# The opening of a three-pass fp32 block kernel: load order, first-unit sums and the places of the side loads

## The chip, the cores and the metric

The kernel runs on one core of a Trainium2 chip. The metric is the device time of one execution in microseconds (us); lower is better. A measurement is the median over several runs.

## The reference

One residual layer with two branches, sequence 1024, width 2048, one batch, all in float32:

```python
mod = einsum('bd,de->be', silu(c), w_ada) + b_ada
shift, scale, gate = split(mod, 3)
h = rms_norm(x, g_pre) * (1 + scale) + shift
proj = einsum('bsd,de->bse', h, w_in)              # 2048 -> 8 x 1024
q, f, i, z, gate_b, gate_c, v_b, z_b = split(proj, 8)
y_a = rms_norm(hgrn2_chunkwise(q, log f, 1 - f, i), g_head) * silu(z)
y_b = gate_b * (causal_conv3(gate_c * v_b) + conv_b) * silu(z_b)
m_a, m_b = split(sigmoid(h @ w_merge + b_merge), 2)
out = (m_a * (y_a @ w_up_a) + m_b * (y_b @ w_up_b)) @ w_o
x = x + gate * rms_norm(out, g_post)
```

## The kernel before

Every large product runs on TensorE (PE) in Strassen-Winograd form, seven half-size products p1 to p7 instead of eight, and each of these as three matmuls of hi and lo float32r parts (`mm3`: hi·hi, hi·lo, lo·hi). The lo parts are made on VectorE (DVE) by `tensor_sub(raw, hi)` after ScalarE (ACT) has copied raw to hi: `split_w` for weights (tiles `w_hi`, `w_lo`), `split_h` for the factors made from h.

**The opening.** x comes in 16 loads of 512 KB, is normalised and transposed into 16 tiles `xT` (channels by sequence). `w_ada`'s scale and shift thirds come in 64 loads of 512 KB (`ada_raw`), 16 for each of four blocks q of 512 channels, in `ada_pair(q)`: the scale half goes through PE (`prow`, 16 matmuls with a one-column weight), the shift half through 16 DVE steps (`row_v`); small matmuls (`pa`) turn both into columns, and DVE makes `a_c` and `sh_c`, which scale and shift `xT`. `factors_a` then makes the factors of p1, p6, p2 and p7 of two channel groups g (tiles `fp`). There are eight groups, and block q feeds groups 2q and 2q+1.

**The first sweep.** 48 units (`unit_a`), each four weight loads of 512 KB (`w_raw`, in 512-byte pieces: a11, a21, a22, a12), sums S1, S2, S4 and a21 (tiles `s` and `w_raw`), and four products of 24 matmuls each: p1 (into `px`), p6 (`py`), p2 (`px` again), p7 (`py` again). `o` takes the results. The POOL queue stores S1 and S4 (`s_scr`, 512 KB each) and `o` (`u_scr`, 768 KB). Beside this run three side jobs: `factors_b` (factors for the second sweep, stored in `hb_scr`), `gate_step` (32 loads `ga_raw` of w_ada's gate third, four DVE steps into `gacc` for two of them) and `sums_o` (32 loads `wo`, sums of w_o stored in `t_scr`).

**The order.** A scheduler of the language places instructions by its own timing model, so a load written late may be issued early, and the other way round; `keep_in_program_order` fixes an instruction in the order in which it is written, and `issue_after` holds a block behind a given instruction. All loads named above stand on the queue of SyncE (SP). An engine takes its instructions strictly in the order in which they stand there. Large tiles share 38 buffers (`big`), the unit weights a ring of five (`raw`). Before the change, every third `ada_raw` load used one of four buffers of its own; the rest used `big`. Unit 0's first two products ran on groups 0 to 5, then 6 and 7; p2 and p7 followed after the last groups were ready.

The rest (second sweep of p5, p4, p3 over 48 units, the two branches, the up projections and the product with w_o) is written the same in both.

Of the kernel before, what the change touches and what calls it, by code (L numbers as in the profile page):

```python
# [26 lines left out]
def tile_hgrn2_shortconv_block(  # L27
# [48 lines left out]
    rows_c = const.tile([16, P], F32, name="rows_c")  # L76
# [1 line left out]
    rows_a = const.tile([80, P], F32, name="rows_a")
    rows_b = const.tile([49, P], F32, name="rows_b")
# [93 lines left out]
    xT = [None] * KT

    def load_x(si):
        for q in range(2):
# [1 line left out]
            nc.sync.dma_start(out=t, in_=x[si * P:(si + 1) * P, q * S:(q + 1) * S])  # L180
# [139 lines left out]
    units = [(w_in_v, (2 * j) * 1024 + i * P, (2 * j + 1) * 1024 + i * P) for i in range(NH) for j in range(4)]  # L320
    units += [(w_merge_v, 256 * m, 256 * m + P) for m in range(16)]

    def load_q(view, par, e0):
        raw = wp.tile([P, 8, P], F32, tag="raw", name="w_raw", bufs=5)
        nc.sync.dma_start(out=raw, in_=view[:, par, :, e0:e0 + P])
        return raw

    def unit_a(u):
        view, e1, e2 = units[u]
        a11, a21 = load_q(view, 0, e1), load_q(view, 0, e2)  # L330
        a22, a12 = load_q(view, 1, e2), load_q(view, 1, e1)
        o = ph.tile([P, 3, HS], F32, tag="o", name="o", bufs=2)
        s1, s2, s4 = (ph.tile([P, 8, P], F32, tag=f"s{n}", name=f"s{n}") for n in (1, 2, 4))
        px, py = ps("mm", "px"), ps("mm", "py")
        w1 = split_w(a11)
        if u:
            product(px, w1, fa["p1"])
        nc.vector.tensor_add(out=s1, in0=a21, in1=a22)
        nc.vector.tensor_sub(out=s2, in0=s1, in1=a11)
        nc.gpsimd.dma_start(out=s_scr[u][:, 0], in_=s1.rearrange("p a b -> p (a b)"))  # L340
        w6 = split_w(s2)
        if u == 0:
            for gs in (range(6), (6, 7)):
                product(px, w1, fa["p1"], pin=True, gs=gs)
                product(py, w6, fa["p6"], pin=True, gs=gs)
        nc.scalar.copy(out=o[:, 2], in_=px)
        if u:
            product(py, w6, fa["p6"])
        nc.vector.tensor_add(out=o[:, 1], in0=o[:, 2], in1=py)
        nc.vector.tensor_sub(out=s4, in0=a12, in1=s2)  # L350
        nc.gpsimd.dma_start(out=s_scr[u][:, 1], in_=s4.rearrange("p a b -> p (a b)"))
        product(px, split_w(a12), fa["p2"], more=True)
        nc.scalar.copy(out=o[:, 0], in_=px)
        nc.vector.tensor_sub(out=a21, in0=a11, in1=a21)
        product(py, split_w(a21), fa["p7"], more=True)
        nc.vector.tensor_add(out=o[:, 2], in0=o[:, 2], in1=py)
        nc.gpsimd.dma_start(out=u_scr[u], in_=o)
# [626 lines left out]
```

## Time and profile before

| | |
|---|---|
| median of 3 runs | 2771.5 us (2767.51 to 2771.66) |
| the profiled execution: time, span | 2769.2 us, 2767.5 us |
| PE busy | 2673.0 us, 97% of the span |
| DVE, ACT, POOL busy | 62%, 33%, 10% |
| opening (to the first product) | 0 to 142.04 us |
| unit 0 | 142.04 to 174.23 us |
| units 1 to 47 | 174.23 to 1213.65 us |

In the rows, L224 is line 224 of the kernel before; an arrow in brackets names what an engine waited for; the DMA share is that of the core's 16 DMA engines.

### The profile page before, as it was taken

How to read it: one execution, taken by the hardware profiler on the slowest of the kernel's cores; microseconds unless marked ns; L12 is line 12 of the kernel's file. 1: busy time of each engine (PE TensorE's matmuls, PEld its weight loads, DVE VectorE, ACT ScalarE, POOL GpSimd, SP SyncE). 2: the span in 40 equal slices, each digit the busy share in tenths (PEclk: the TensorE clock that was granted, in tenths of full speed). 3: DMA queues.
4: the chain of work that ended last, by engine and by line, in shares of the span. 5: the costliest groups of instructions: out<-in, count | busy, mean ns of one | idle time of the engine just before them, and what ended most of it. 6: DMA issues, size and time to landing. Idle time of an engine off the chain costs nothing.

```text
span 2767.5 us, 31307 instructions
## 1 busy us (share of the span) xinstructions
PE 2673.0 (97%) x11851; PEld 2152.7 (78%) x11851; DVE 1716.7 (62%) x2096; ACT 906.3 (33%) x1176; POOL 280.0 (10%) x495
## 2 busy tenths in 40 slices
PE   4889999999999999999999999999998999999997
PEld 3267878888888888888888888888885787888786
DVE  6777886754554444546666666656563666765667
ACT  4433222222222222233344444435442222232333
POOL 2012111110000000010000000002111101100000
PEclk9899999999999999999999999999998999999999
DMA  9769999985556655584444444359999569773353
GB/s 361 286 201 313 345 349 364 346 292 179 179 192 179 182 175 177 174 316 137 133 130 133 138 146 138 110 178 374 360 363 407 187 213 335 235 282 99 99 178 142
DMA packets 420071, 631.30 MB, mean 228 GB/s; under 512 B 19564, under 2 KB 281808, under 8 KB 419792
## 3 DMA queue, kind: packets, MB, share of 16 engines
q1 hardware_dynamic: 358528, 394.31, 44.7%
q0 software_dynamic: 60208, 230.78, 21.7%
q10 hardware_dynamic: 1184, 4.20, 0.4%
q8 instruction: 93, 1.52, 0.2%
q14 instruction: 58, 0.48, 0.0%
HBM read 431.04 MB, written 198.18 MB: 227 GB/s over the span
## 4 chain that ended last, share of the span: by engine, by line
PE 81%; issue 8%; DMA 7%; DVE 2%; POOL 1%; ACT 1%; DVEq 0%; POOLq 0%; ACTq 0%; SPq 0%
PE po L866 10%; PE pz L119 7%; PE pz L122 7%; PE pz L123 7%; PE px L119 6%; PE px L123 6%; PE px L122 6%; PE py L123 6%; PE py L119 6%; PE py L122 6%; PE pw L119 4%; PE pw L122 4%; PE pw L123 4%; DMA yp<-yf_scr 3%; DMA ga_raw<-in_w_ada_dram 2%
## 5 line engine op out<-in xcount | busy, mean ns | idle before, releaser
L130 ACT CAST w_hi<-w_raw 128x1024 fp32r<-128x1024 f32 (+1 forms) x296 | 290.9, 983 | 1001.6 <-PE px L122 402.5
L131 DVE TENSOR_TENSOR w_lo<-w_raw,w_hi 128x1024 fp32r<-128x1024 f32 (+1 forms) x296 | 335.7, 1134 | 273.1 <-ACT w_hi L130 263.4
L123 PE MATMUL py<-fp,w_lo 128*128 128x512 f32 x768 | 301.2, 392 | 6.9 <-DVE w_lo L131 6.9
L123 PE MATMUL px<-fp,w_lo 128*128 128x512 f32 x768 | 300.9, 392 | 5.2 <-DVE w_lo L131 5.2
L119 PE MATMUL px<-fp,w_hi 128*128 128x512 f32 x768 | 301.2, 392 | 0.0
L122 PE MATMUL py<-fp,w_hi 128*128 128x512 f32 x768 | 299.5, 390 | 1.3 <-DVE fp L136 1.3
L119 PE MATMUL py<-fp,w_hi 128*128 128x512 f32 x768 | 299.8, 390 | 0.9 <-ACT w_hi L130 0.9
L122 PE MATMUL px<-fp,w_hi 128*128 128x512 f32 x768 | 300.0, 391 | 0.0
L866 PE MATMUL po<-w_hi,lt 128*128 128x512 f32 x896 | 244.2, 390 | 0.6 <-DVE og L900 0.6
L866 PEld LDWEIGHTS po<-w_hi,lt 128*128 128x128 f32 x896 | 168.1, 188 | 37.2 <-DVE og L900 2.2
L130 ACT CAST w_hi<-s 128x512 fp32r<-128x512 f32 (+1 forms) x112 | 90.1, 805 | 285.9 <-PE py L122 245.5
L123 PEld LDWEIGHTS py<-fp,w_lo 128*128 128x128 f32 x768 | 144.5, 188 | 41.5 <-DVE w_lo L131 11.2
L123 PEld LDWEIGHTS px<-fp,w_lo 128*128 128x128 f32 x768 | 144.8, 188 | 36.9 <-DVE w_lo L131 6.5
L122 PEld LDWEIGHTS py<-fp,w_hi 128*128 128x128 f32 x768 | 144.5, 188 | 32.1 <-DVE fp L136 1.7
L122 PEld LDWEIGHTS px<-fp,w_hi 128*128 128x128 f32 x768 | 145.1, 189 | 30.8 <-issue 0.5
L119 PEld LDWEIGHTS px<-fp,w_hi 128*128 128x128 f32 x768 | 144.9, 189 | 30.8 <-issue 0.7
L119 PEld LDWEIGHTS py<-fp,w_hi 128*128 128x128 f32 x768 | 144.5, 188 | 30.8 <-ACT w_hi L130 1.3
L119 PE MATMUL pz<-fp,hi 128*128 128x512 f32 x384 | 152.5, 397 | 3.0 <-DVE d L701 3.0
L122 PE MATMUL pw<-fp,w_hi 128*128 128x512 f32 x384 | 150.8, 393 | 0.0
L119 PE MATMUL pz<-fp,w_hi 128*128 128x512 f32 x384 | 150.5, 392 | 0.0
L123 PE MATMUL pz<-fp,lo 128*128 128x512 f32 x384 | 150.4, 392 | 0.0
L119 PE MATMUL pw<-fp,w_hi 128*128 128x512 f32 x384 | 150.4, 392 | 0.0
(286 smaller groups left out, 4959.4 us busy)
## 6 DMA issues: line engine op xcount, KB each, us to landing
w_raw<-in_w_in_dram SPq DMA_DIRECT2D x160, 512.0 KB, 5.2
s_scr<-s POOLq DMA_DIRECT2D x96, 512.0 KB, 6.0
s_raw<-s_scr SPq DMA_DIRECT2D x96, 512.0 KB, 4.3
w_raw<-in_w_merge_dram SPq DMA_DIRECT2D x80, 512.0 KB, 5.7
u_scr<-o POOLq DMA_DIRECT2D x48, 768.0 KB, 7.5
ada_raw<-in_w_ada_dram SPq DMA_DIRECT2D x64, 512.0 KB, 10.8
yf_scr<-yp POOLq DMA_DIRECT2D x56, 512.0 KB, 9.0
yp<-yf_scr SPq DMA_DIRECT2D x56, 512.0 KB, 12.8
```

What stands on the lines that cost most here:

```text
L119: mm = nc.tensor.matmul(o, ah, bh, start=first, stop=False, skip_group_check=True)
L122: nc.tensor.matmul(o, ah, bl, start=False, stop=False, skip_group_check=True)
L123: nc.tensor.matmul(o, al, bh, start=False, stop=last, skip_group_check=True)
L130: nc.scalar.copy(out=hi, in_=raw)
L131: nc.vector.tensor_sub(out=lo, in0=raw, in1=hi.bitcast(F32))
L866: nc.tensor.matmul(o, a, b[:, c], start=st, stop=sp, skip_group_check=True)
```

## The change

In words: (1) a helper `load` pins the loads of x, `ada_raw`, the weights of units 0 and 1, `ga_raw` and `wo` in the order in which they are written. (2) All `ada_raw` loads of blocks 0 to 2 and three of four of block 3 use the 38 large buffers; the pool of their own falls from four to two, and small tiles (`rows_a`, `rows_b`, `rows_c`, `row_p`) share others, which pays for the memory. (3) Unit 0's loads, its S1, S2, a21 and the splits of a11, S2 and a12 (`hi3a`, `lo3a`) are written ahead of block 3's `ada_pair`; p1, p6 and p2 of unit 0 run over groups 0 to 5, then 6 and 7; its S4, p7 and stores are issued after `factors_a((6, 7))`. p2 has a PSUM tile of its own there. (4) `factors_b`, `gate_step` and `sums_o` move: `factors_b(u/2 - 1)` at units 2, 4, ... 16, issued after that unit's last sum; two gate steps at each of units 10 to 25 (before 16 to 31); `sums_o` at 26, 28, ... 40 (before 32 to 46), with the loads pinned, so that they can no longer be issued many units earlier.

```diff
+    def load(o, i):
+        tc.keep_in_program_order(nc.sync.dma_start(out=o, in_=i))
...
     def ada_load(t, q, k):
         n_ada[0] += 1
-        if n_ada[0] % 3:
+        if q < 3 or n_ada[0] % 4:
             raw = bigt(F32, "ada_raw").rearrange("p (k e) -> p k e", k=2)
         else:
-            raw = ph.tile([P, 2, HS], F32, tag="ada", name="ada_raw", bufs=4)
-        nc.sync.dma_start(out=raw, in_=w_ada_v[:, k:k + 2, t, q * HS:(q + 1) * HS])
+            raw = ph.tile([P, 2, HS], F32, tag="ada", name="ada_raw", bufs=2)
+        load(raw, w_ada_v[:, k:k + 2, t, q * HS:(q + 1) * HS])
         return raw
...
+    def unit_a(u, raws):
...
+        if u == 0:
+            v.tensor_sub(out=a21, in0=a11, in1=a21)
+            w2 = split_w(a12, out_t=(ph.tile([P, 8, P], F32R, name="hi3a", bufs=1), wp.tile([P, 8, P], F32R, tag="raw", name="lo3a", bufs=5)))
+            yield
+            p2 = ps("mm", "p2")
+            for gs in (range(6), (6, 7)):
+                for p, w, f in ((px, w1, "p1"), (py, w6, "p6"), (p2, w2, "p2")):
+                    product(p, w, fa[f], pin=True, gs=gs)
...
     for q in range(1, 4):
+        if q == 3:
+            first = unit_a(0, load_a(0))
+            next(first)
         ada_pair(q)
         factors_a((2 * q - 2, 2 * q - 1))
-    factors_a((6, 7), vec=(7,))
+    with tc.issue_after(factors_a((6, 7), vec=(7,)).ins):
+        next(first, None)
...
     for u in range(NU):
-        unit_a(u)
-        if u < 16:
-            if u % 2 == 0:
-                factors_b(u // 2)
-        elif u < 32:
-            gate_step(2 * u - 32)
-            gate_step(2 * u - 31)
-        elif u % 2 == 0:
-            sums_o((u - 32) // 2)
+        if u:
+            for _ in unit_a(u, load_a(u)):
+                pass
+        if u in range(2, 18, 2):
+            with tc.issue_after(last_sum[0]):
+                factors_b(u // 2 - 1)
+        if 10 <= u < 26:
+            gate_step(2 * u - 20)
+            gate_step(2 * u - 19)
+        elif u in range(26, 42, 2):
+            sums_o((u - 26) // 2)
```

What moves, on the engines that wait or are waited for. First SP's queue in the opening, before (each row is one kind of load, "x60" sixty in a row):

```order
L180 DMA x_0_427<-in_x_dram 128x1024
L180 DMA x_1_429<-in_x_dram 128x1024
L224 DMA ada_raw<-in_w_ada_dram 128x2x512 x4
L325 DMA w_raw<-in_w_in_dram 128x8x128 x5
L224 DMA ada_raw<-in_w_ada_dram 128x2x512 x60
L325 DMA w_raw<-in_w_in_dram 128x8x128 x21
```

and after:

```order
L119 DMA x_1_428<-in_x_dram 128x1024
L119 DMA ada_raw<-in_w_ada_dram 128x2x512 x48
L119 DMA w_raw<-in_w_in_dram 128x8x128 x4
L119 DMA ada_raw<-in_w_ada_dram 128x2x512 x16
L119 DMA w_raw<-in_w_in_dram 128x8x128 x4
L311 DMA w_raw<-in_w_in_dram 128x8x128 x45
L119 DMA ga_raw<-in_w_ada_dram 128x2x512
```

Five unit loads stood ahead of 60 `ada_raw` loads; now four stand ahead of the last 16. Within the 60, the order before was the scheduler's, and is the written one now.

Second, DVE around `a_c` of the last block (the last `row_v` step is the shift's; `a_c` needs PE's `pa`), before:

```order
L239 SCALAR_TENSOR_TENSOR row_v<-ada_raw,c_act,row_v 128x512 x6
L247 TENSOR_TENSOR a_c<-pa,cols 128x4
L249 TENSOR_TENSOR sh_c<-pa,cols 128x4
L338 TENSOR_TENSOR s_1184<-w_raw 128x1024
L248 SCALAR_TENSOR_TENSOR a_c<-a_c,cols 128x4
L339 TENSOR_TENSOR s_1185<-s_1184,w_raw 128x1024
L354 TENSOR_TENSOR w_raw<-w_raw 128x1024
L266 TENSOR_SCALAR xT_570<-xT_570,a_c,sh_c 128x1024
```

and after, where the sums stand a whole block earlier, right behind `a_c` of block 2 and among the first `row_v` steps of block 3:

```order
L252 SCALAR_TENSOR_TENSOR a_c<-a_c,cols 128x4
L331 TENSOR_TENSOR s_1025<-w_raw 128x1024
L332 TENSOR_TENSOR s_1026<-s_1025,w_raw 128x1024
L336 TENSOR_TENSOR w_raw<-w_raw 128x1024
L241 TENSOR_SCALAR row_v<-ada_raw,c_act 128x512
L134 TENSOR_TENSOR lo3a<-w_raw,hi3a 128x1024
L243 SCALAR_TENSOR_TENSOR row_v<-ada_raw,c_act,row_v 128x512
L134 TENSOR_TENSOR w_lo<-s_1026,w_hi 128x1024
```

Third, DVE in one of units 20 to 24, before (L338, L339, L350 and L354 are S1, S2, S4 and a21, L131 the lo parts of p6, p2, p7 and the next p1):

```order
L338 TENSOR_TENSOR s_4537<-w_raw 128x1024
L356 TENSOR_TENSOR o<-o,py 128x512
L354 TENSOR_TENSOR w_raw<-w_raw 128x1024
L131 TENSOR_TENSOR w_lo<-s_4393,w_hi 128x1024
L339 TENSOR_TENSOR s_4538<-s_4537,w_raw 128x1024
L350 TENSOR_TENSOR s_4539<-w_raw,s_4538 128x1024
L131 TENSOR_TENSOR w_lo<-w_raw,w_hi 128x1024
L349 TENSOR_TENSOR o<-o,py 128x512
L131 TENSOR_TENSOR w_lo<-w_raw,w_hi 128x1024 x2
```

and after, where units 21 to 23 read alike and 20 and 24 add the last sums of a gate block (the lines are now L331, L332, L347, L355 and L134, and L397 is a gate step):

```order
L331 TENSOR_TENSOR s_4597<-w_raw 128x1024
L357 TENSOR_TENSOR o<-o,py 128x512
L355 TENSOR_TENSOR w_raw<-w_raw 128x1024
L134 TENSOR_TENSOR w_lo<-s_4452,w_hi 128x1024
L332 TENSOR_TENSOR s_4598<-s_4597,w_raw 128x1024
L397 SCALAR_TENSOR_TENSOR gacc<-ga_raw,c_act,gacc 128x512
L347 TENSOR_TENSOR s_4599<-w_raw,s_4598 128x1024
L397 SCALAR_TENSOR_TENSOR gacc<-ga_raw,c_act,gacc 128x512
L134 TENSOR_TENSOR w_lo<-w_raw,w_hi 128x1024
L397 SCALAR_TENSOR_TENSOR gacc<-ga_raw,c_act,gacc 128x512 x2
L346 TENSOR_TENSOR o<-o,py 128x512
L134 TENSOR_TENSOR w_lo<-w_raw,w_hi 128x1024 x2
```

Four gate steps have come in, the first of them between S2 and S4. On SP's queue after, the two `ga_raw` loads of such a unit stand directly behind four `w_raw` loads, so behind a12, which waits for S1; the four `wo` loads later stand in the same place:

```order
L119 DMA ga_raw<-in_w_ada_dram 128x2x512 x2
L311 DMA w_raw<-in_w_in_dram 128x8x128 x4
L119 DMA wo<-in_w_o_dram 128x2x512 x4
L311 DMA w_raw<-in_w_in_dram 128x8x128 x8
L119 DMA wo<-in_w_o_dram 128x2x512 x4
```

Before, the `ga_raw` loads stood between single `w_raw` loads from the 26th after the opening on, well ahead of the gate steps.

## Rows read from the trace of the kernel before

**Rows 1.** The page: span, busy time of the engines.

```profile
span 2767.5 us, 31307 instructions
PE 2673.0 (97%) x11851; PEld 2152.7 (78%) x11851; DVE 1716.7 (62%) x2096; ACT 906.3 (33%) x1176; POOL 280.0 (10%) x495
```

**Rows 2.** PE's timeline, opening to unit 1: start, length, idle before in brackets.

```profile
72.14 3.57 PE L235 MATMUL prow<-ada_raw,c_act 128*1 128x512 f32 x4 [15.64 <-DMA ada_raw<-in_w_ada_dram]
...
136.10 3.38 PE L235 MATMUL prow<-ada_raw,c_act 128*1 128x512 f32 x4 [2.75 <-DMA ada_raw<-in_w_ada_dram]
140.15 1.05 PE L244 MATMUL pa<-ones,row_p 1*128 1x1 f32 x8 [0.66 <-ACT row_p L240]
...
142.04 0.48 PE L119 MATMUL px<-fp,w_hi 128*128 128x512 f32 x1
...
174.23 0.39 PE L119 MATMUL px<-fp,w_hi 128*128 128x512 f32 x1
```

**Rows 3.** DMA from 0 to 160 us: GB/s in 40 slices of 4 us.

```profile
GB/s 145 297 417 412 410 409 386 337 291 313 386 387 386 388 387 388 386 387 209 255 61 72 254 159 371 360 397 387 387 386 387 385 387 209 0 4 201 299 49 238
```

**Rows 4.** A wait of SP's queue, 0 to 142 us: total, times, longest.

```profile
SPq L224 <- PE prow L235: 14.8, 6, 5.3
```

**Rows 5.** DVE's timeline around the last a_c.

```profile
139.03 0.75 DVE L239 SCALAR_TENSOR_TENSOR row_v<-ada_raw,c_act,row_v 128x512 f32<-128x512 f32 x1
142.22 0.16 DVE L247 TENSOR_TENSOR a_c<-pa,cols 128x4 f32<-128x4 f32 x1 [2.43 <-PE pa L244]
...
145.89 0.81 DVE L266 TENSOR_SCALAR xT<-xT,a_c,sh_c 128x1024 f32<-128x1024 f32 x1
...
148.66 1.28 DVE L278 TENSOR_TENSOR xT<-keep,xT 128x512 f32<-128x512 f32 x2
```

**Rows 6.** Unit 0: busy time and clock; then PE's waits.

```profile
142.04:174.23 32.19, 26.05 (x98) 20.14 (x98) 26.80 (x36) 12.59 (x19) 2.73 (x5) 0.89 0.52 160
PE py L123 <- DVE w_lo L131: 2.7, 1, 2.7
PE px L123 <- DVE w_lo L131: 2.2, 1, 2.2
PE py L122 <- DVE fp L136: 1.3, 1, 1.3
```

**Rows 7.** Windows: 12 late units, then units 1 to 47.

```profile
696.50:957.60 261.10, 260.88 (x1150) 215.24 (x1149) 128.91 (x120) 61.41 (x72) 19.19 (x36) 1.00 0.59 179
174.23:1213.65 1039.42, 1031.27 (x4522) 848.19 (x4521) 617.67 (x621) 256.20 (x306) 121.99 (x229) 1.00 0.76 249
```

**Rows 8.** One late unit: PE, then SP, POOL and DVE.

```profile
754.93 0.39 PE L119 MATMUL px<-fp,w_hi 128*128 128x512 f32 x1
760.83 0.39 PE L123 MATMUL py<-fp,w_lo 128*128 128x512 f32 x1
766.27 0.39 PE L123 MATMUL px<-fp,w_lo 128*128 128x512 f32 x1
757.16 0.37 SPq L325 DMA_DIRECT2D w_raw<-in_w_in_dram  x1
758.26 0.53 POOL L357 DMA_DIRECT2D u_scr<-o  x1 [0.30 <-issue]
758.78 1.22 DVE L131 TENSOR_TENSOR w_lo<-s,w_hi 128x1024 fp32r<-128x1024 f32 x1
762.10 1.23 DVE L350 TENSOR_TENSOR s<-w_raw,s 128x1024 f32<-128x1024 f32 x1 [0.84 <-DMA w_raw<-in_w_in_dram]
```

**Rows 9.** Gate steps before: PE and DMA, 260 to 380 us; the loads' median time.

```profile
260.00:380.00 120.00, 116.97 (x509) 95.08 (x508) 99.19 (x119) 29.06 (x35) 14.60 (x27) 1.00 1.03 344
ga_raw<-in_w_ada_dram SPq DMA_DIRECT2D x31, 512.0 KB, 8.4
```

**Rows 10.** A wait of PE followed by the lower clock, unit 2.

```profile
227.77 0.69 PE L123 MATMUL py<-fp,w_lo 128*128 128x512 f32 x1 [1.98 <-DVE w_lo L131]
...
228.69 0.63 PE L122 MATMUL py<-fp,w_hi 128*128 128x512 f32 x1
```

More of the change, by code (lines that the diff above doesn't have):

```diff
@@ L75, in tile_hgrn2_shortconv_block @@
     make_identity(nc, ident)
[L76 removed]
+    rows = wp.tile([P, S], F32, tag="raw", name="rows", bufs=5)
+    rows_a, rows_b, rows_c = rows[0:80, 0:P], rows[0:49, P:2 * P], rows[0:16, 2 * P:3 * P]
     nc.scalar.dma_start(out=rows_c, in_=c[0].rearrange("(n p) -> n p", p=P))
[L78 to L79 removed]
     b_rows = b_ada[0].rearrange("(n p) -> n p", p=P)
@@ L135, in split_h @@
         eng(out=t[:, 0], in_=raw)
-        nc.vector.tensor_sub(out=t[:, 1], in0=raw, in1=t[:, 0].bitcast(F32))
+        return nc.vector.tensor_sub(out=t[:, 1], in0=raw, in1=t[:, 0].bitcast(F32))
     STAGES = ("p1", "p6", "p2", "p7", "p5", "p4", "p3")
@@ L179, in load_x @@
             t = bigt(F32, f"x_{si}_{q}")
-            nc.sync.dma_start(out=t, in_=x[si * P:(si + 1) * P, q * S:(q + 1) * S])
+            load(t, x[si * P:(si + 1) * P, q * S:(q + 1) * S])
             xrow[si][q] = t
@@ L229, in ada_pair @@
         prow = ps("aux", "prow")
-        row_p, row_v = (ph.tile([P, HS], F32, tag=t, name=t) for t in ("row_p", "row_v"))
+        row_p, row_v = o0[:, 0], ph.tile([P, HS], F32, tag="row_v", name="row_v")
         for k in range(0, KT, 2):
@@ L272, in keep_f @@
             fa[s][g] = pair(f"f{s}_{g}")
-            split_h(fa[s][g], raw, nc.scalar.copy)
+            return split_h(fa[s][g], raw, nc.scalar.copy)
         for g, b11, b12, b21, b22 in parts:
@@ L283, in factors_a @@
         for g, b11, b12, b21, b22 in parts:
-            keep_f("p7", g, b12)
+            last = keep_f("p7", g, b12)
+        return last
     def factors_b(g):
@@ L299, in factors_b, with load_q, load_a @@
             nc.gpsimd.dma_start(out=hb_scr[n][g], in_=t.rearrange("p a b -> p (a b)").bitcast(F32))
+    units = [(w_in_v, (2 * j) * 1024 + i * P, (2 * j + 1) * 1024 + i * P) for i in range(NH) for j in range(4)]
+    units += [(w_merge_v, 256 * m, 256 * m + P) for m in range(16)]
+    def load_q(view, par, e0, pin=False):
+        raw = wp.tile([P, 8, P], F32, tag="raw", name="w_raw", bufs=5)
+        (load if pin else nc.sync.dma_start)(raw, view[:, par, :, e0:e0 + P])
+        return raw
+    def load_a(u):
+        view, e1, e2 = units[u]
+        return [load_q(view, *a, pin=u < 2) for a in ((0, e1), (0, e2), (1, e2), (1, e1))]
@@ new lines, in tile_hgrn2_shortconv_block @@
+    last_sum = [None]
+    def unit_a(u, raws):
+        a11, a21, a22, a12 = raws
+        o = ph.tile([P, 3, HS], F32, tag="o", name="o", bufs=2) if u else o0
+        s1, s2 = (ph.tile([P, 8, P], F32, tag=f"s{n}", name=f"s{n}", bufs=1) for n in (1, 2))
+        s4 = ph.tile([P, 8, P], F32, tag="s4", name="s4") if u else s1
+        px, py = ps("mm", "px"), ps("mm", "py")
+        v = nc.vector
+        w1 = split_w(a11)
+        if u:
+            product(px, w1, fa["p1"])
+        v.tensor_add(out=s1, in0=a21, in1=a22)
+        v.tensor_sub(out=s2, in0=s1, in1=a11)
+        nc.gpsimd.dma_start(out=s_scr[u][:, 0], in_=s1.rearrange("p a b -> p (a b)"))
+        w6 = split_w(s2)
+        if u == 0:
[6 more added lines that the diff above has]
+                    product(p, w, fa[f], pin=True, gs=gs)
+        nc.scalar.copy(out=o[:, 2], in_=px)
+        if u:
+            product(py, w6, fa["p6"])
+        v.tensor_add(out=o[:, 1], in0=o[:, 2], in1=py)
+        v.tensor_sub(out=s4, in0=a12, in1=s2)
+        nc.gpsimd.dma_start(out=s_scr[u][:, 1], in_=s4.rearrange("p a b -> p (a b)"))
+        if u:
+            product(px, split_w(a12), fa["p2"], more=True)
+            nc.scalar.copy(out=o[:, 0], in_=px)
+        else:
+            v.tensor_add(out=o[:, 0], in0=o[:, 2], in1=p2)
+        if u:
+            v.tensor_sub(out=a21, in0=a11, in1=a21)
+        product(py, split_w(a21), fa["p7"], more=True)
+        last_sum[0] = v.tensor_add(out=o[:, 2], in0=o[:, 2], in1=py).ins
+        nc.gpsimd.dma_start(out=u_scr[u], in_=o)
@@ L318, in tile_hgrn2_shortconv_block @@
     ph = ph_pool.__enter__()
[L320 to L357, printed above, removed]
     gacc = [None]
@@ L364, in gate_step @@
         raw = bigt(F32, "ga_raw").rearrange("p (k e) -> p k e", k=2)
-        nc.sync.dma_start(out=raw, in_=w_ada_v[:, 2 * kq:2 * kq + 2, 2, eb * HS:(eb + 1) * HS])
+        load(raw, w_ada_v[:, 2 * kq:2 * kq + 2, 2, eb * HS:(eb + 1) * HS])
         if kq == 0:
@@ L390, in sums_o @@
         for t, par, c in ((b12, 0, 1), (b22, 1, 1), (b11, 0, 0), (b21, 1, 0)):
-            nc.sync.dma_start(out=t, in_=w_o_v[:, par, g, :, c, :])
+            load(t, w_o_v[:, par, g, :, c, :])
         v = nc.vector
```

2 lines of the change are left out of this document (added).

## The prediction

> **What bounds the kernel now.** I read the page first: PE is busy for 2673.0 of 2767.5 us [rows 1], so a gain can only come from the places where PE is idle or at the lower of its two clocks, 1.2 in place of 2.4 GHz. PE's timeline shows these places: all of the opening up to the first product at 142.04, and unit 0, which ends at 174.23 [rows 2]. Then the windows: twelve late units take 261.10 us, 21.76 each and with PE never idle for long, while units 1 to 47 take 1039.42, which is 16.8 more than 47 x 21.758 = 1022.6 [rows 7]. The changed lines reach no further than unit 47, and the instructions after it stay nearly in their order, so the sum has three terms: opening, unit 0, units 1 to 47.
>
> In the opening the DMA line is the view to look at [rows 3]: it should stand at some 387 GB/s as long as there is something to load, and in the six slices from 72 to 96 us it reads 209, 255, 61, 72, 254, 159. PE shows why: it waits 15.64 us, up to 72.14, for one scale load of block 1, whose matmuls it takes in order [rows 2], though loads for later steps were already there and held their buffers. SP's queue then waits for PE to free buffers, 14.8 us in six waits [rows 4].
>
> **The change, part by part.** *Load order.* The six slices moved 1010 x 4 = 4.04 MB where 6 x 387 x 4 = 9.29 MB could have moved; the missing 5.25 MB are 13.6 us at 387. With the loads in the order in which PE and DVE take them, and more of the large buffers, I expect this hole to close. Four unit loads instead of five stand ahead of the last block; one takes 1.8 us (524 KB at 291 GB/s, the slices from 32 to 40 where they ran). The store of unit 0's S1 now falls into the opening, 1.4 us (524 KB at 387). So the last `ada_raw` lands at 136.1 - 13.6 - 1.8 + 1.4 = 122.1 instead of 136.1.
>
> Can the engines follow? A block of 16 loads is 21.7 us of DMA. DVE needs for it 16 steps of 0.75 and 12 factor steps of 0.64 [rows 5], 19.7 us. Block 3 adds the six steps of unit 0 at 1.22 [rows 8], 27.0 in all, against 21.7 + 4 x 1.8 = 28.9. It fits, with 2 us to spare; that is the cover of the sums, and what they go beyond it would be paid one for one.
>
> *From the last load to the first product.* Before, 5.9 us: 3.4 of matmuls at the lower clock, 0.66 for ACT's copy, 1.9 of `pa` [rows 2]. In written order the last scale load lands one load, 1.4 us, ahead of the last shift load. At the full clock (1.7 for the matmuls) this gives 2.9 us behind the last load, at the lower one 4.6. I take 3.3, since the loads come evenly and PE is busy for two thirds of the time there. First product at 125.4, a gain of 16.6. The bounds are 20 (no hiccup at all) and 3 (the hole stays).
>
> *Unit 0.* It takes 32.2 us now, 10.4 above a late unit: 6.2 in three waits on DVE [rows 6], the rest the clock (mean 0.89). After, its sums are done before `a_c`. Groups 0 to 5 of three products are 54 matmuls, 54/96 of 21.76 = 12.2 us. Under these DVE makes the last two groups' factors: the columns 0.4, three scaling steps 1.6, 12 steps of 0.64, in all 9.7 [rows 5]. So the three waits go; if the cover were gone the whole 9.7 would stand in front of groups 6 and 7. I leave one stretch at the lower clock in (1.7): 23.5 us, a gain of 8.7. Unit 1 would begin 25.3 us earlier.
>
> *The sweep.* Before, the gate loads were issued far ahead and the side jobs spent most of the 16.8 us in units 2 to 12. After, I sum what is late in each unit; X is the start of its p1.
> - Unit 1: DVE's order puts unit 0's last sum, which needs the end of p7, ahead of unit 1's first lo part: 0.64 + 1.22, less the 0.45 that PE's first two matmuls cover, 1.4.
> - `factors_b` now starts behind a unit's last sum and puts two steps, 1.28, ahead of p6's lo part in some seven units. That part ends at 760.00 and is wanted at 760.83 [rows 8], so 0.45 remain of each: 3.2.
> - Its stores fall beside the load of a22 in units 4 and 6. No row before has this alone; bounds are nothing and a wait like that of unit 2, 1.98 [rows 10]. I take 1.5 each, nearer to that wait because the DMA share is high there: 3.0.
> - Gate units 20 to 24: a12 is issued at X + 2.2 and in at X + 7.2 [rows 8], and the first gate load stands right behind it. At the full rate it follows by 1.4, at half of it (beside the stores of POOL, issued at X + 3.3) by 2.7: X + 8.6 to 9.9, say 9.2. DVE takes strictly in order a gate step, S4, a gate step and p2's lo part, 0.75 + 1.23 + 0.75 + 1.22 = 3.9 with small overlaps 3.7. PE gets the lo part at X + 12.9 and wants it at X + 11.3 [rows 8]: 1.6 late, bounds 1.0 and 2.3. Five units: 7.8.
> - Gate units 10 to 19: here the steps are spread over the unit. Before, with six gate loads for each unit and all of them early, PE lost 3.0 us in 120 [rows 9], 0.55 for each unit. I take 0.6, ten times 6.0; bounds nothing and 1.6 each.
> - What I expect to stand as before (the gate's own small matmuls, scattered waits): an estimate of a third of the 16.8, 5.4.
> - The wait in unit 2 was followed by the lower clock (0.63 for a matmul [rows 10], 0.39 elsewhere [rows 8]). Unit 0's mean clock of 0.89 makes 3.5 us of its 32.2 [rows 6], lost in two such stretches, so 1.7 each. I allow for two: 3.4.
>
> Together 30.2, 13.4 more than before. The side loads for w_o stand behind a12 as well, but their sums come after p2's lo part and have some four us until p7's is due: nothing.
>
> **Sum.** -16.6 - 8.7 + 13.4 = -11.9, from the profiled execution's 2769.2 to 2757.3. That execution lay 2.3 below the median of 2771.5, so the forecast is 2760.
>
> On the half rate the Trainium skill has a rule: its page "DMA: Bandwidth & Descriptors", section "Queues, rings and completion order", says that each DMA engine goes round its queues packet by packet, so two busy queues would share it evenly. By that rule the gate loads come at the late end in every gate unit, and the sum would be that of the second rival, 2783. The trace agrees only in part: a12 was there 4.9 us after its issue with a store of 768 KB under way [rows 8].
>
> **The rivals.**
> First, *the gate loads are hidden anyway*: if the first of them lands by X + 7.5, DVE loses nothing in units 10 to 25. For it: a12 itself takes only 4.9 us, and the DMA share of a late unit is 0.59 [rows 7]. Against it: it can't be issued before a12, whose buffer waits for S1. The sweep then loses 30.2 - 13.8 - 1.7 = 14.7, and the time is 2744.
>
> Second, *the gate loads eat the gain*, the slower side: all 16 gate units stall as units 20 to 24 do at the late end. Their loads, held to their units, share each unit's worst stretch with a12 and 1.2 MB of stores. The two first terms gain 25.3, and the sweep without these units loses 16.4 where it lost 16.8 before; so the balance is at 25.7 for the 16 units, 1.6 for each. At 2.3 each they cost 36.8 in place of 13.8, and the time is 2783. For it: the 8.4 us that gate loads took before [rows 9]. Against it: 8.4 was with the DMA engines full.
>
> Third, *the opening doesn't gain*: the change doesn't do what it says, since buffers run out all the same (the 16 `xT` tiles and the factors hold most of the 38 by block 3) or DVE is short by more than its 2 us. Then the 13.6 us come back, and -11.9 + 13.6 gives 2773. Against it: the hole stands at blocks 1 and 2, when fewer factors are there.
>
> **How the numbers follow.** The forecast has 0.57, the first rival 0.15, the second 0.12, the third 0.13, other mishaps 0.03. The forecast's own range is 2751 to 2769, from the bounds of the gate units and of the opening. The range 2744 to 2777 reaches to the first and the third rival and leaves out the second. A measurement of this kernel can tell about 0.2%, 5.5 us, from no change. Faster by more holds in nine tenths of the forecast and in the first rival: 0.66. Within it are the rest of the forecast and most of the third: 0.20. Slower: 0.14.
>
> **What would show it.** Right: the DMA line at some 387 without a hole from 40 to 115 us; the last `prow` matmuls near 121 and the first product near 125; unit 0 without a wait on `w_lo` and near 23.5 us; the first gate step of units 20 to 24 waiting for `ga_raw`, and PE waiting 1 to 2 us for p2's `w_lo` there. Wrong: a second hole in the DMA line in block 3, a wait of PE between groups 5 and 6 of unit 0, gate units of 21.8 us, or waits there above 2 us each followed by the lower clock.

## The result, and the profile after

The changed kernel is slower: 2800.7 us (median of 4 runs, 2798.31 to 2808.02) beside 2769.5 for the kernel before in the same series (2763.51 to 2771.66), a ratio of 1.0127 with a 95% interval of 1.0109 to 1.0144. The forecast was 2760, and its range ended at 2777.

The profiled execution of the changed kernel took 2798.3 us. Its page, to be read beside [rows 1]:

```profile
span 2796.6 us, 31303 instructions
PE 2683.6 (96%) x11851; PEld 2151.1 (77%) x11851; DVE 1716.2 (61%) x2097; ACT 905.5 (32%) x1175; POOL 280.1 (10%) x495
...
PE 58%; DMA 16%; issue 10%; DVE 8%; POOL 2%; ACT 1%; SPq 1%; DVEq 0%; POOLq 0%; ACTq 0%
```

DVE works as long as before, and PE has 10.6 us more of busy time for the same 11851 matmuls: 16.0 more in units 1 to 47, less in the opening and in unit 0. The span is 29.1 longer. The last line is the chain that ended last: a sixth of it is DMA, where it was 7% before.

The DMA line of the opening, 0 to 160 us in slices of 4, answers to [rows 3]; PE's timeline then to [rows 2], DVE's to [rows 5]:

```profile
GB/s 149 318 410 410 410 409 387 388 384 389 384 386 388 386 387 388 384 388 384 376 389 387 332 287 351 390 388 397 172 393 301 151 0 4 0 6 252 27 240 123
```

```profile
121.56 2.89 PE L239 MATMUL prow<-ada_raw,c_act 128*1 128x512 f32 x4 [0.34 <-DMA ada_raw<-in_w_ada_dram]
...
129.57 1.87 PE L248 MATMUL pa<-ones,row_v 128*128 128x1 f32 x8 [3.42 <-DVE row_v L243]
131.30 0.77 PE L122 MATMUL px<-fp,w_hi 128*128 128x512 f32 x1
...
156.37 0.39 PE L122 MATMUL px<-fp,w_hi 128*128 128x512 f32 x1
...
103.84 0.16 DVE L251 TENSOR_TENSOR a_c<-pa,cols 128x4 f32<-128x4 f32 x1 [0.83 <-PE pa L248]
...
126.40 3.11 DVE L243 SCALAR_TENSOR_TENSOR row_v<-ada_raw,c_act,row_v 128x512 f32<-128x512 f32 x4
131.48 0.16 DVE L251 TENSOR_TENSOR a_c<-pa,cols 128x4 f32<-128x4 f32 x1 [1.96 <-PE pa L248]
```

The hole of 72 to 96 us is closed, and the last scale load is in by 121.56, near the 121 that was forecast. One slice, 112 to 116 us, still reads 172: SP's queue waits there for DVE to free buffers. A wait of SP's queue, 0 to 131 us:

```profile
SPq L119 <- DVE row_v L243: 22.6, 8, 9.5
```

`pa` waits 3.42 us for DVE's `row_v`, and the first product stands at 131.30: 10.7 earlier than before, not 16.6. Unit 0 ends at 156.37.

Windows: unit 0, units 1 to 47, block 3 in DVE's time, and a stretch of unit 23 (columns: length, busy PE, PEld, DVE, ACT, POOL, granted clock, DMA share, GB/s):

```profile
131.30:156.40 25.10, 25.04 (x98) 20.11 (x99) 13.22 (x22) 9.66 (x14) 0.54 (x1) 0.88 0.29 84
...
156.40:1242.85 1086.45, 1047.22 (x4521) 848.44 (x4520) 623.50 (x631) 256.50 (x307) 123.58 (x231) 0.99 0.74 240
...
103.84:131.48 27.64, 20.06 (x49) 5.35 (x48) 24.50 (x37) 12.11 (x17) 0.60 (x1) 0.81 0.77 263
...
680.00:683.40 3.40, 3.40 (x9) 2.64 (x8) 1.67 (x2) 0.00 (x0) 0.00 (x0) 0.50 0.59 167
```

Units 1 to 47 take 1086.45, which is 63.8 more than 47 x 21.758 = 1022.6; before it was 16.8 [rows 7]. 39.2 of them PE was idle, and 24.6 it was busy beyond the 1022.6 (8.7 before). Of the 24.6 the granted clock explains 6.8: it stands at its lower level in four short stretches, at 509, 680, 888 and 1059 us, and at the full clock elsewhere. Most of the rest, some 13 by PE's timeline, stands at the waits themselves: a matmul of 0.39 us begins 0.23 after the one ahead of it, but the last one ahead of a wait ends without this overlap, and the next begins some 0.34 after the first behind it. Unit by unit (from one p1 to the next): unit 1 loses 2.0, units 2 to 9 4.3, 10 to 19 13.8, 20 to 24 17.3 (27.2, 23.2, 24.1, 26.1, 25.4 us), units 25 to 40, which hold the w_o sums, 25.9, and the rest 0.5. The amount of side traffic alone doesn't do it: in the kernel before the w_o loads and sums stood in units 9 to 18, some four in each, no sum waited for its load, and units 10 to 19 lost 2.7. From the end of unit 47 on both kernels take the same, 1553.8 and 1553.9. So: opening -10.7, unit 0 -7.1, sweep +47.0, together +29.2.

The waits of units 1 to 47 (total, times, longest):

```profile
DVE s L331 <- DMA w_raw<-in_w_in_dram: 113.1, 29, 6.5
DVE s L331 <- DMA w_raw<-in_w_merge_dram: 82.0, 16, 6.9
...
DVE gacc L397 <- DMA ga_raw<-in_w_ada_dram: 35.3, 14, 5.4
DVE wo L416 <- DMA wo<-in_w_o_dram: 30.8, 8, 5.8
PE px L126 <- DVE w_lo L134: 24.9, 15, 2.6
...
PE py L126 <- DVE w_lo L134: 10.1, 21, 1.4
```

PE waits for lo parts, 36 times. DVE itself waits for gate and w_o loads, and far longer, 195 us in 45 waits, for unit weights: L331 is S1 = a21 + a22 of the next unit. How a gate step's wait reaches PE is seen in unit 23, DVE's timeline and then PE's, with the step (L397) ahead of p2's lo part (L134, at 677.26):

```profile
674.80 0.75 DVE L397 SCALAR_TENSOR_TENSOR gacc<-ga_raw,c_act,gacc 128x512 f32<-128x512 f32 x1 [3.73 <-DMA ga_raw<-in_w_ada_dram]
...
678.54 0.50 PE L126 MATMUL px<-fp,w_lo 128*128 128x512 f32 x1 [2.49 <-DVE w_lo L134]
```

Here is how S1's wait reaches PE, at the border of two units with w_o work (SP and POOL issue, DVE and PE work; rows by engine):

```profile
1014.88 0.39 PE L122 MATMUL px<-fp,w_hi 128*128 128x512 f32 x1
...
1028.33 0.50 PE L126 MATMUL px<-fp,w_lo 128*128 128x512 f32 x1 [1.23 <-DVE w_lo L134]
...
1015.86 0.37 SPq L311 DMA_DIRECT2D w_raw<-in_w_merge_dram  x1
...
1008.27 0.53 POOL L421 DMA_DIRECT2D t_scr<-wo  x1 [5.17 <-DVE wo L416]
...
1014.99 0.53 POOL L421 DMA_DIRECT2D t_scr<-wo  x1 [0.73 <-DVE wo L419]
1016.96 0.53 POOL L358 DMA_DIRECT2D u_scr<-o  x1 [1.44 <-issue]
...
1014.61 1.22 DVE L134 TENSOR_TENSOR w_lo<-w_raw,w_hi 128x1024 fp32r<-128x1024 f32 x1
...
1016.34 1.22 DVE L134 TENSOR_TENSOR w_lo<-s,w_hi 128x1024 fp32r<-128x1024 f32 x1
1023.52 1.23 DVE L331 TENSOR_TENSOR s<-w_raw 128x1024 f32<-128x1024 f32 x1 [5.96 <-DMA w_raw<-in_w_merge_dram]
...
1027.06 1.22 DVE L134 TENSOR_TENSOR w_lo<-w_raw,w_hi 128x1024 fp32r<-128x1024 f32 x1
```

A unit begins at 1014.88. At 1015.83 DVE has finished p1's lo part (1014.61 + 1.22), which frees one of the five weight buffers, and at 1015.86 SP issues a22 of the *next* unit into it. POOL has issued four stores of `t_scr` since 1008.27, three of them are still under way, one of `u_scr` follows at 1016.96, and a22 is in only at 1023.4, 7.5 us after its issue. DVE has S1 of the next unit in its queue *ahead* of the running unit's p2 lo part; it stands still for 5.96 us, then does S1, S2 and a21, and only at 1027.06 the lo part that PE's p2 wants at 1027.1. PE stops for 1.23; had a22 taken 6.3 us, it would not have stopped.

In the kernel before, S1 stood one lo part further forward, ahead of p6's, with almost no slack; a row of its trace (DVE's timeline in the late unit of [rows 8]) shows it:

```profile
755.90 1.23 DVE L338 TENSOR_TENSOR s<-w_raw 128x1024 f32<-128x1024 f32 x1 [4.12 <-DMA w_raw<-in_w_in_dram]
```

S1 waits 4.12 us for a22, which comes with no other transfer beside it (issued 751.81, landed 755.78), and p6's lo part, three steps behind S1 at 758.78, ends 0.83 ahead of its use [rows 8]. In that place whatever delays a22 by more than 0.83 goes to PE.

### The profile page after: what moved, and what is told of

Read it like the earlier page. It is cut to its first block, busy times and chain, and to the rows that moved or that the text cites. A ratio compares the mean times of both kernels' runs of the same rounds, so it can differ in the third digit from the quotient of the medians.

```text
span 2796.6 us, 31303 instructions
## 1 busy us (share of the span) xinstructions
PE 2683.6 (96%) x11851; PEld 2151.1 (77%) x11851; DVE 1716.2 (61%) x2097; ACT 905.5 (32%) x1175; POOL 280.1 (10%) x495
## 4 chain that ended last, share of the span: by engine, by line
PE 58%; DMA 16%; issue 10%; DVE 8%; POOL 2%; ACT 1%; SPq 1%; DVEq 0%; POOLq 0%; ACTq 0%
PE po L891 10%; PE pz L122 5%; PE pz L126 5%; PE pz L125 5%; DMA w_raw<-in_w_in_dram 4%; PE px L122 4%; PE px L126 4%; PE px L125 4%; PE py L126 3%; PE py L122 3%; PE py L125 3%; DMA wo<-in_w_o_dram 3%; DVE w_lo L134 3%; DMA yp<-yf_scr 3%; PE pw L122 3%
## 5 line engine op out<-in xcount | busy, mean ns | idle before, releaser
L134 DVE TENSOR_TENSOR w_lo<-w_raw,w_hi 128x1024 fp32r<-128x1024 f32 (+1 forms) x295 | 334.9, 1135 | 238.6 <-ACT w_hi L133 236.6
L331 DVE TENSOR_TENSOR s<-w_raw 128x1024 f32<-128x1024 f32 x48 | 58.8, 1225 | 195.1 <-DMA w_raw<-in_w_in_dram 113.1
```

What stands on the lines that cost most here:

```text
L134: nc.vector.tensor_sub(out=lo, in0=raw, in1=hi.bitcast(F32))
L331: v.tensor_add(out=s1, in0=a21, in1=a22)
```

## The experiments

Twelve kernels ran, in four groups, each group on one chip beside the kernel before; ratios are to the kernel before of the same group (medians 2765.9, 2766.7, 2765.9 and 2767.1). "Loss" is the time from the first product to the end of unit 47, less 48 x 21.76; it is 27.1 before and 67.1 after.

### Which part of the change costs the time

**e1_opening_only**: the changed opening and unit 0, with the loop of the kernel before and gate and w_o loads not pinned. **e2_side_jobs_only**: the other half, the kernel before with this loop and the pinned loads:

```diff
+        if u in range(2, 18, 2):
+            with tc.issue_after(last_sum[0]):
+                factors_b(u // 2 - 1)
+        if 10 <= u < 26:
+            gate_step(2 * u - 20)
+            gate_step(2 * u - 19)
+        elif u in range(26, 42, 2):
+            sums_o((u - 26) // 2)
```

Expected of e1: 

> The opening and unit 0 as in the changed kernel, the side jobs at their places before, their loads not pinned. Theory A (the loss sits in the side jobs, wherever the opening begins): the traces put the opening at -10.7 us and unit 0 at -7.1, so about 18 us below the kernel before, 2748 to 2755. Theory B (the new opening itself upsets the sweep, by a shifted phase of loads and buffers): the sweep keeps much of its 47 us, so not below the kernel before.

Measured: 2763.5, ratio 0.999 (0.998 to 1.0). First product at 131.43, loss 30.1. Half right: the loss stays near that of before, but the 18 us of opening and unit 0 come back only in part; units 1 to 47 lose some 27 where they lost 16.8, and unit 47 ends at 1206.1 instead of 1213.7. The side jobs of the first units, begun earlier, now meet units 0 to 9; PE's timeline has one wait of 5.26 us there, for a copy by ACT that stands behind one of `factors_b`:

```profile
161.88 0.80 PE L122 MATMUL px<-fp,w_hi 128*128 128x512 f32 x1 [5.26 <-ACT w_hi L133]
```

Expected of e2: 

> The opening of the kernel before, with only the side jobs of the changed kernel (new places, gate and w_o loads pinned). Theory A: the loss of the sweep comes with them, so 40 to 50 us above the kernel before, 2810 to 2820. Theory B: near the kernel before.

Measured: 2807.1, ratio 1.014 (1.012 to 1.0161), loss 68.0. The loss comes with the side jobs, whatever the opening.

**e3_not_pinned**: the changed kernel, where only this differs (and the same for `wo`):

```diff
-        load(raw, w_ada_v[:, 2 * kq:2 * kq + 2, 2, eb * HS:(eb + 1) * HS])
+        nc.sync.dma_start(out=raw, in_=w_ada_v[:, 2 * kq:2 * kq + 2, 2, eb * HS:(eb + 1) * HS])
```

> The changed kernel with its gate and w_o loads not pinned; the side jobs are written at the same places, so the scheduler issues the w_o loads some five units earlier and their sums with them, while the gate loads of units 10 to 17 stand where they stood. If the pin of the w_o loads is to blame for units 25 to 40 (26 us), these go and the time is 2765 to 2778. If the places in the code are to blame, it stays at 2795 to 2800.

Measured: 2759.8, ratio 0.9976 (0.9965 to 0.9987), loss 25.5. The w_o units lose next to nothing (1.5 in units 25 to 40), gate units 10 to 19 lose 14.2. The scheduler spreads the w_o sums one by one over units 21 to 29.

### Explanations that fall short

**e4_steps_behind_p2**: loads pinned as in the change, but gate steps and w_o sums held behind p2's lo part of their unit, so that no side step that waits for its load stands ahead of it.

```diff
+            lo_p2[0] = last_lo[0]
...
+        if jobs:
+            with tc.issue_after(lo_p2[0]):
+                for j in jobs:
+                    next(j, None)
```

> The changed kernel with the same pinned loads at the same places, but the DVE steps that use them (gate steps, w_o sums) issued only behind the lo part of p2 of the unit in which they are written, which is about a unit later than now. Theory 1 (DVE's queue: a step that waits for a late side load stands ahead of a lo part, and PE and the weight loads wait for that): units 20 to 40 lose 43 us now and should lose 10 at most, so 2758 to 2770. Theory 2 (DMA crowd: the held loads make the weight loads themselves late, whatever DVE does): at least half of the 43 us stays, 2780 or more.

Measured: 2784.1, ratio 1.006 (1.0042 to 1.0078), loss 53.0. Gate units 20 to 24 lose 1.0 together and 10 to 19 8.6; units 25 to 47 still lose some 35. There no w_o sum waits for its load any more, so waiting side steps are not the cause. The trace shows S1 at its longest wait, ahead of p6's lo part (L134, at 982.89):

```profile
980.01 1.23 DVE L334 TENSOR_TENSOR s<-w_raw 128x1024 f32<-128x1024 f32 x1 [9.07 <-DMA w_raw<-in_w_merge_dram]
```

Its a22 was issued at 970.97 and landed at 979.89, beside `t_scr` stores issued from 964.7 to 969, three of them still under way. So I suspected the burst of stores, or the pinned burst of w_o loads, and tried each alone on e4: **e5_stores_two_and_two** issues two of the four stores a unit later, with the order of POOL's stores fixed (its w_o loads then slip between weight loads); **e6_wo_loads_free** takes the pin from the w_o loads.

```diff
+            if n == 2:
+                yield
+            tc.keep_in_program_order(nc.gpsimd.dma_start(out=t_scr[n][g], in_=t.rearrange("p a b -> p (a b)")))
```

> The kernel of e4 with the four stores of a w_o sum split: two at their place, two held on POOL's queue until the S4 store of the next unit; the scheduler also lets two of the four w_o loads slip between the next weight loads. In e4 units 26 to 41 still lose some 35 us, and in its trace a22 takes 8.9 us in a unit with the four stores of 512 KB, 4 to 6 in one without. Theory S (the burst of stores delays a22): the loss halves or better, 2758 to 2770. Theory L (the four loads behind a12 do it): as e6. Neither: stays at 2780.

> The kernel of e4 with only the w_o loads not pinned: two of four slip between weight loads, the sums and the burst of four stores stay behind p2's lo part. Theory L (the bunch of loads behind a12): the 35 us of units 26 to 41 go for the most part, 2752 to 2762. Theory S (the burst of stores): they stay, 2775 to 2785.

Measured: e5 2784.8, ratio 1.0057 (1.004 to 1.0074), loss 58.1; e6 2807.3, ratio 1.0147 (1.0132 to 1.0162), loss 71.2. Both were missed. In e6 the w_o loads are issued among the next unit's weight loads, and the odd units from 31 to 41 take 28.4 to 30.3; a22 takes 11.5 us (issued 986.11, landed 997.62), and S1 and PE wait longer than in any other run. A wait of e6, units 0 to 47, and the row of that S1:

```profile
PE px L126 <- DVE w_lo L134: 35.5, 12, 6.8
```

```profile
997.70 1.23 DVE L334 TENSOR_TENSOR s<-w_raw 128x1024 f32<-128x1024 f32 x1 [8.78 <-DMA w_raw<-in_w_merge_dram]
...
1001.23 1.22 DVE L134 TENSOR_TENSOR w_lo<-w_raw,w_hi 128x1024 fp32r<-128x1024 f32 x1
```

**e7_gate_held_wo_free**: the gate as in e4, w_o as in e3.

> The best version that the runs so far point to: the gate loads pinned and their steps behind p2's lo part as in e4, the w_o sums as in e3 (not pinned, not held). The gate units 10 to 25 lost 9 us in e4 against 14 in e3, the w_o units nothing in e3; so 4 to 6 us below e3, 2752 to 2757, if the two are independent; at e3's 2760 or above if the w_o sums, now later than in e3, meet the just-in-time loads of units 24 to 35.

Measured: 2763.5, ratio 0.9992 (0.9983 to 1.0002), loss 28.7. Not below e3, as in the second alternative: units 10 to 19 lose 8.6 where e3 loses 14.2, but the w_o sums come later and unit 26 alone loses 8.0, with seven w_o loads in it and three sums and S1 ahead of p2's lo part, for which PE waits 6.28 us.

### The opening

**e8_sums_behind_a_c**: the changed kernel with unit 0's sums and splits held behind the last `a_c`, out of block 3.

```diff
+        done = ada_pair(q)
+        if q == 3:
+            first = unit_a(0, raws0)
+            with tc.issue_after(done.ins):
+                next(first)
```

> The changed kernel with unit 0's six sums and splits held behind a_c of the last block, its loads where they are. Theory D (DVE bounds the opening: in the changed kernel PE waits 3.4 us for the row of the shift, while the last load is in by 122): a_c and the first product come 4 to 6 us earlier, 125 to 127, and unit 0 is longer by as much or more, since its sums then stand in front of the factors. Theory M (the loads still bound it): first product at 131 as now. The total stays within 5 us of the changed kernel, 2795 to 2805.

Measured: 2793.3, ratio 1.0094 (1.0079 to 1.0109). The first product comes at 126.17, 5.1 earlier, so DVE did set the end of the opening:

```profile
126.17 0.77 PE L122 MATMUL px<-fp,w_hi 128*128 128x512 f32 x1
```

But unit 1 starts at 155.7 where it started at 156.4: unit 0 takes 29.5 us instead of 25.1, since the same DVE work now stands inside it. The place of the sums is worth 0.7 us, which is less than traces differ: in those of the other kernels with the changed opening unit 1 starts between 156.4 and 158.3.

### What the weight loads' lack of slack costs

Both failed explanations treat what delays a22. The remaining one, theory J, treats what stands behind it: S1 waits in DVE's queue ahead of lo parts that don't need it. Three kernels move S1 of the next unit behind p2's lo part of the running one, and the next S4 behind the next p1's lo part, with all loads, stores and sums kept: **e9_s1_behind_p2** on the changed kernel, **e10_s1_and_steps_behind_p2** on e4, **e11_s1_behind_p2_not_pinned** on e3.

```diff
         w1 = split_w(a11)
+        lo_p1 = last_lo[0]
...
-        v.tensor_add(out=s1, in0=a21, in1=a22)
+        with tc.issue_after(lo_p2[0]) if u > 1 else nullcontext():
+            v.tensor_add(out=s1, in0=a21, in1=a22)
...
-        v.tensor_sub(out=s4, in0=a12, in1=s2)
+        with tc.issue_after(lo_p1) if u > 1 else nullcontext():
+            v.tensor_sub(out=s4, in0=a12, in1=s2)
```

> The changed kernel, with its loads pinned as they are, but from unit 2 on S1 of the next unit held behind p2's lo part of the running one, and the next S4 behind the next p1's lo part. In the changed kernel S1 stands ahead of p6's and p2's lo parts and waits there for a22 (in one w_o unit 7.5 us from issue to landing). Theory J (the weight loads are just in time, and what stalls PE is that S1 waits ahead of the lo parts): the w_o units fall from some 3 us of loss each to under 0.5, the gate units 20 to 24 to under 1; loss of the sweep after unit 0 some 20 in place of 64; end of the sweep near 1199, time 2752 to 2760. Theory V (a w_o unit moves too much for the DMA engines, whatever the order of DVE): units 26 to 41 still lose 25, and the time stays at 2790 to 2800.

> The same hold of S1 and S4, and the gate steps and w_o sums held behind p2's lo part too, as in e4_steps_behind_p2 (2784, units 26 to 41 losing some 32). Theory J: as the run before within 3 us, 2751 to 2760, units 20 to 25 at 21.8. Theory V: as e4, 2780 to 2788, since the loads and stores of a unit are the same. If e9 stays slow and this one is fast, the waiting side steps were a cause of their own besides S1.

> The hold of S1 and S4 on the version with the loads of gate and w_o not pinned (e3_not_pinned, 2760, loss of the sweep 25.5 of which some 14 in units 12 to 21, none in the w_o units). Theory J: gate units 12 to 21 lose half of the 14, time 2751 to 2757. Theory V, or if those units lose by DVE's own work (gate steps and factors_b together) rather than by a wait for weights: 2758 to 2762, as e3.

Measured: e9 2757.4, ratio 0.9967 (0.9954 to 0.9979), loss 23.8; e10 2754.1, 0.9955 (0.994 to 0.997), loss 23.5; e11 2747.7, 0.9928 (0.9914 to 0.9942), loss 14.6. Theory V falls: the same traffic in units with the same work, in another order on DVE, takes 43 us less. By groups, e9 loses 4.8 in units 10 to 19 (13.8 after the change), 0.9 in 20 to 24 (17.3) and 13.1 in 25 to 40 (25.9); the last is more than theory J said. The hold moves more than S1 and S4, though: in e9's trace the gate steps of units 20 to 24 that wait and the first w_o sums stand behind p7's lo part, where they stood ahead of p2's and p7's. So e9 alone doesn't part S1 from the side steps. The pair e4 and e10 does, since both hold the side steps: with S1 and S4 held as well, units 25 to 47 lose 8.1 in place of 35.2, and the time falls by 30 us, from 2784.1 to 2754.1. That is theory J's cause. The waits of units 1 to 47 in e9, where L336 is S1 and L404 and L423 are the side steps:

```profile
DVE wo L423 <- DMA wo<-in_w_o_dram: 39.9, 8, 6.0
DVE gacc L404 <- DMA ga_raw<-in_w_ada_dram: 34.2, 18, 6.1
DVE s L336 <- DMA w_raw<-in_w_merge_dram: 7.2, 4, 6.0
DVE s L336 <- DMA w_raw<-in_w_in_dram: 7.0, 3, 3.9
PE px L126 <- DVE w_lo L134: 6.0, 5, 3.0
...
PE py L126 <- DVE w_lo L134: 1.0, 3, 0.3
```

S1's waits fall from 195 us to 14, PE's for lo parts from 35 to 7, and DVE waits as long as after the change for the side loads, now at little cost. The same stretch of a w_o unit in e9, DVE's timeline (p2's lo part, S1, p7's lo part and a w_o sum):

```profile
963.41 1.23 DVE L134 TENSOR_TENSOR w_lo<-w_raw,w_hi 128x1024 fp32r<-128x1024 f32 x1 [4.21 <-ACT w_hi L133]
964.55 1.22 DVE L336 TENSOR_TENSOR s<-w_raw 128x1024 f32<-128x1024 f32 x1
...
968.85 1.23 DVE L134 TENSOR_TENSOR w_lo<-w_raw,w_hi 128x1024 fp32r<-128x1024 f32 x1
976.03 1.23 DVE L423 TENSOR_TENSOR wo<-wo 128x1024 f32<-128x1024 f32 x1 [5.95 <-DMA wo<-in_w_o_dram]
```

p2's lo part now waits for ACT's hi part alone, that is for nothing late; DVE's 5.95 us for w_o lie between p7's lo part and the next p1's, where there is nearly room: PE waits 0.56 us at 979.84. A load of w_merge takes 7.6 us in the median of e9's whole run, longer than the 6.1 after the change.

Two units of e9 still lose 4.6 and 4.7, units 32 and 40. In the first, a22 takes 13.3 us (issued 842.62, landed 855.96), and S1, now behind p2's lo part, holds up the next ones in the queue instead, o and p7's lo part; in the other, two w_o sums stand ahead of the next p1's lo part, and it is them that wait, 8.5 us. DVE's timeline in the first, then PE's wait:

```profile
856.09 1.23 DVE L336 TENSOR_TENSOR s<-w_raw 128x1024 f32<-128x1024 f32 x1 [6.02 <-DMA w_raw<-in_w_merge_dram]
...
859.62 0.68 DVE L351 TENSOR_TENSOR o<-o,py 128x512 f32<-128x512 f32 x1
...
860.45 0.47 PE L122 MATMUL py<-fp,w_hi 128*128 128x512 f32 x1 [1.62 <-DVE o L351]
```

So the hold gives S1 more room, not all that it would need.

The intervals of e10 and e9 overlap, so a hold of the side steps is worth a few us at most on top of that of S1. In e10 units 32 and 40 lose 0.0 and 1.7, but units 18 and 41 lose 5.5 and 5.4; in unit 41 S1 waits 7.71 us ahead of `o` and p7's lo part, as in the first of these two.

**e12_before_s1_behind_p2**: the same hold in the kernel before.

> The kernel before with the same hold: S1 of the next unit behind p2's lo part, the next S4 behind the next p1's lo part; opening and side jobs as before. If the hold only mends what the change broke (theory J as far as it goes), there is little to mend: the late units of before lose nothing, most of its 16.7 us of loss stand in units 1 to 12 and hang on gate loads and factors_b, so 2762 to 2769, the same within 0.2 per cent, and what e9 to e11 gain over it is the opening and unit 0. If the order of S1 cost something in every unit with side work, before too, its sweep loses some 8 less: 2754 to 2760.

Measured: 2757.5, ratio 0.9966 (0.9954 to 0.9979), loss 18.0. The second alternative: the order that the hold changes cost the kernel before some 9 us too, most of it in units 2 to 9, which lose 5.6 instead of 12.2. The waits of units 1 to 47 for S1, first in the kernel before, then in e12:

```profile
DVE s L338 <- DMA w_raw<-in_w_merge_dram: 77.6, 16, 5.3
DVE s L338 <- DMA w_raw<-in_w_in_dram: 58.1, 18, 5.3
```

```profile
DVE s L343 <- DMA w_raw<-in_w_in_dram: 10.5, 4, 5.1
```

With the hold on both sides, e11 against e12 is what opening and unit 0 and the new places of the side jobs are worth when they don't starve the lo parts: 0.9928 / 0.9966 = 0.996, some 10 us. e11, at 2747.7, beats both kernels.

## Why the prediction was wrong

**Opening, -16.6; it was -10.7.** Load order and the closing of the hole were right, and the last loads came within 1.6 us (scale 121.5 beside 120.7, shift 123.7 beside 122.1). The step that failed is "It fits, with 2 us to spare". 27.0 us of DVE work for block 3 were set against 28.9 counted in loads; but DVE begins block 3 only after block 2's `a_c`, at 103.84, when the last load of block 2 had been in for 12.6 us (landed 91.28), and 27.64 later it has block 3's. The work was sized a little high (24.5 busy); its start was not the start of the loads. What it goes beyond was "paid one for one", as the sentence after it says, and e8 shows the other side: without the six steps the first product is at 126.17, within 0.8 of the forecast 125.4.

**Unit 0, -8.7; it was -7.1.** The waits on `w_lo` are gone, and PE is busy for 25.04 of 25.10 us. Of the remaining 3.3 above 21.76 the clock makes 3.0 (0.88 granted), where 1.7 was allowed.

**Sweep, +13.4; it was +47.0.** This is the error that decides. By the terms of the sum: unit 1 2.0 (1.4), `factors_b` and its stores 4.3 (6.2), gate units 20 to 24 17.3 (7.8), 10 to 19 13.8 (6.0), w_o units 25.9 ("nothing"); the allowances for what stands as before and for the clock (8.8) are contained in these. A third of the 16.8 is 5.6 and not 5.4, which changes nothing.

The largest miss is the term priced at nothing, with the sentence that "their sums come after p2's lo part and have some four us until p7's is due". Both halves of it failed. The cover of the sums was overrun: the first sum of a unit waits 3.3 to 5.8 us for its load, and PE waits behind such sums in seven of units 25 to 39, 5.2 us in all. The longest, in unit 39, DVE's timeline and then PE's (`o` stands right behind the sum):

```profile
1056.60 1.23 DVE L416 TENSOR_TENSOR wo<-wo 128x1024 f32<-128x1024 f32 x1 [5.75 <-DMA wo<-in_w_o_dram]
...
1058.57 0.49 PE L122 MATMUL py<-fp,w_hi 128*128 128x512 f32 x1 [2.40 <-DVE o L346]
```

And the sentence looked at the sums alone. S1 of the next unit was never priced, though its wait of 4.12 us stood in the trace before with 0.83 of slack behind it; the side traffic delays a22, S1 holds up DVE, and PE waits behind it for 10.2 us in units 25 to 40. The experiments bear out both: e4, in which no sum waits, takes 14 off the loss of 67, and e10, which moves S1 and S4 besides, 30 more. The bunch comes from the pin: e3, written the same but with free loads, spreads the sums and loses 1.5 in units 25 to 40.

In the gate units the mechanism was right and its size wrong. In units 20 to 24 a gate step between S2 and S4 waits 3.2 to 3.8 us for its load, and PE waits 1.1 to 2.6 us for p2's lo part, 10.6 in all, against a forecast of 7.8; 1.4 stand behind S1 in unit 20, and the rest of the 17.3 is PE's longer busy time around the waits, 1.7 of it the lower clock. e4, which holds the gate steps behind p2's lo part and leaves S1, loses 1.0 there. In units 10 to 19 the steps were not "spread over the unit": they came in batches of 6 to 14 in units 12, 14, 16 and 18, which lose 1.9 to 3.8 each where 0.6 was taken.

**The rivals.** The second pointed the right way, with a time of 2783 and the gate loads as the cause; the time was worse, and 26 of the 64 us came from w_o. The third was right in its second half (DVE short), at 5.9 us instead of 13.6. The 0.14 for slower was too little: the forecast summed edits that were each hidden by slack, and never asked what slack the weight loads themselves had.

**The half rate.** The prediction's 4.9 us are a12's from its issue to S4, and two stores were under way, not one: S1's of 512 KB too, from 757.42. a22 took 4.0 us with no other transfer beside it (751.81 to 755.78 in the kernel before), 7.5 in the unit above, 8.9 in e4 and 11.5 in e6. The Trainium skill's page "DMA: Bandwidth & Descriptors", section "Queues, rings and completion order", says that each engine goes round its queues packet by packet; beside stores the direction agrees. At half of 387 GB/s the 0.52 MB would take 1.4 us more than at the full rate, which is an estimate by that rule; the trace has 3.5, 4.9 and 7.5 more, the last of them mostly beside loads of the same queue, so the size doesn't follow from it, and no run here takes it apart further.

**What stays open.** Why e11 is 10 us below e9 is argued, not shown: its loads are not pinned, and units 25 to 40 lose 0.1 where e9 loses 13.1; gate units 10 to 24 lose 9.4 against 5.7. The 13.1 of e9 there and the places that the scheduler chose for the side steps were not tried apart. How much of e1's lost gain stands in each of units 1 to 9 was not tried.

## What to carry to other kernels

Before a load or a store is put into a stage, look in that stage for the instructions that wait longest for their data, even where the wait costs nothing today, and read what is queued behind them on the same engine and with how much slack; that slack, not the DMA share, is what new traffic may use. An instruction for the next round should stand behind those of the running round that don't need it. And a budget of work against loads needs the time at which the engine can begin, besides the two lengths.

## What the runs showed of the hardware

A 512 KB load in 512-byte pieces took 4.0 us with no other transfer beside it (kernel before, 751.81 to 755.78), 4.8 beside two stores (757.16 to 761.97), 7.5 beside four stores and the end of another load (after, 1015.86 to 1023.40), and 11.5 beside five loads of its own queue and a store (e6, 986.11 to 997.62); the third at a mean of 305 GB/s (995 to 1024 us), below the 387 of the opening. And short waits of PE cost more than their length: 39.2 us of idle time in units 1 to 47 came with 24.6 us of busy time beyond the 1022.6 of the late units, of which the lower clock makes 6.8; in e9, where the idle time is 9.2, with 11.8 (1034.38 busy in 1043.61), of which the lower clock makes 3.4.
